# The last stores of a SiLU-multiply kernel, issued from SP instead of from ACT's queue

## The chip, the cores and the metric

The kernel runs on one core of a Trainium2 chip. The metric is the device time of one execution, in microseconds (us); lower is better. The span in a profile is some 1.8 us shorter than that time (470.1 against 471.92 us in the profiled run of before). Executions of one kernel differ by up to 0.8 us, so effects of some tenths of a us are read from the trace and not from the time.

Four names are used throughout. **ACT** is ScalarE and **DVE** is VectorE. **SP** is SyncE, which here only issues DMAs. A **ring** is the queue of transfers that one issuing engine has on the DMA engines: q1 in the profile belongs to SP, q10 to ACT.

## The reference

```python
def reference(x):                     # x: (32, 512, 2048) float32
    half_dim = x.shape[-1] // 2
    x1, x2 = x[..., :half_dim], x[..., half_dim:]
    return x1 * (1 / (1 + np.exp(-x1))) * x2      # (32, 512, 1024) float32
```

It reads 134.2 MB, writes 67.1 MB, and does one activation and one multiply per output.

## The kernel before

The rows are cut into 16 tiles of 8 MB in and 4 MB out. Two input and two output buffers exist. A tile is computed in four pieces of 2 rows per partition; its result is stored whole, except in the last tile, where each piece is stored as soon as it is done.

```python
    K, KC = 8, 2
    ...
    def load(i):
        xt = in_pool.tile([P, K, in_cols], dt, name="xt")
        nc.sync.dma_start(out=xt, in_=xv[i])
        loaded[i] = xt

    load(0); load(1)
    for i in range(n_tiles):
        xt = loaded.pop(i)
        last = i == n_tiles - 1
        ot = out_pool.tile([P, K, half], dt, name="ot")
        for c in range(0, K, KC):
            ce = c + KC
            nc.scalar.activation(out=ot[:, c:ce, :], in_=xt[:, c:ce, :half],
                                 func=mybir.ActivationFunctionType.Silu)
            nc.vector.tensor_mul(out=ot[:, c:ce, :], in0=ot[:, c:ce, :],
                                 in1=xt[:, c:ce, half:])
            if last:
                nc.scalar.dma_start(out=ov[i][:, c:ce, :], in_=ot[:, c:ce, :])
        if not last:
            nc.scalar.dma_start(out=ov[i], in_=ot)
        if i + 2 < n_tiles:
            load(i + 2)
```

The framework may reorder instructions of one engine where data allows it. In the program that results, ACT's queue holds for the last tile: activations 0 to 2, the stores of pieces 0 to 2, activation 3, the store of piece 3.

Of the kernel before, what the change touches and what calls it, by code (L numbers as in the profile page):

```python
# [1 line left out]

# [4 lines left out]


@with_exitstack
def kernel(  # L10
    ctx: ExitStack,
    tc: tile.TileContext,
    x: bass.AP,
    out: bass.AP,
):





    nc = tc.nc
    P = nc.NUM_PARTITIONS

    x_flat = x.flatten_outer_dims()
    out_flat = out.flatten_outer_dims()
    num_rows, in_cols = x_flat.shape
    half = in_cols // 2
    dt = x_flat.dtype

    K = 8  # L30
    KC = 2
    n_tiles = num_rows // (P * K)
    assert n_tiles * P * K == num_rows

    in_pool = ctx.enter_context(tc.tile_pool(name="in_pool", bufs=2))
    out_pool = ctx.enter_context(tc.tile_pool(name="out_pool", bufs=2))

    xv = x_flat.rearrange("(n p k) d -> n p k d", p=P, k=K)
    ov = out_flat.rearrange("(n p k) d -> n p k d", p=P, k=K)

    loaded = {}
# [6 lines that stand above are left out]
    load(0)  # L48
    load(1)
# [6 lines that stand above are left out]
            nc.scalar.activation(  # L56
                out=ot[:, c:ce, :],
                in_=xt[:, c:ce, :half],
                func=mybir.ActivationFunctionType.Silu,
            )  # L60
            nc.vector.tensor_mul(  # L61
                out=ot[:, c:ce, :],
                in0=ot[:, c:ce, :],
                in1=xt[:, c:ce, half:],
            )
            if last:
                nc.scalar.dma_start(out=ov[i][:, c:ce, :], in_=ot[:, c:ce, :])  # L67
        if not last:
            nc.scalar.dma_start(out=ov[i], in_=ot)
        if i + 2 < n_tiles:  # L70
            load(i + 2)


# [1 line left out]
_INS = ['x']  # L75
_OUTS = [((32, 512, 1024), 'float32')]


# [23 lines left out]
```

## Time and profile before

| what | value |
|---|---|
| time, median of 4 runs | 471.92 us (471.72 to 472.5) |
| bytes moved, mean rate | 201.35 MB, 428 GB/s |
| last load lands | 451.97 us from the span's start |
| previous tile's 4 MB store (the "old store") lands | 459.23 us |
| the last tile's pieces land | 461.65, 464.08, 466.51, 469.23 us |
| compute of the last tile ends (multiply 3) | 465.34 us |

Lines of the page of before: span; busy time of the engines; the busy tenths of the DMA engines in 40 slices of the span; the chain that ended last, by engine.

```profile
span 470.1 us, 267 instructions
...
DVE 142.4 (30%) x64; ACT 118.3 (25%) x65; POOL 0.2 (0%) x4
...
DMA  8999999999999999999999999999999999999998
...
DMA 80%; DVE 15%; ACT 4%; issue 0%; ACTq 0%; SPq 0%
```

The DMA engines are at nine tenths or more in 38 of 40 slices. That is the limit of this kernel: the compute engines are idle 70% and 75% of the time. Note the chain's 15% DVE: it means that the chain of releases passes through DVE, not that a faster DVE would help as long as the DMA engines always have other work.

The tail in the timeline of before (start, duration, engine, line, operation, tiles; in brackets the idle time before it and what ended it; ACTq is ACT's sequencer issuing a DMA):

```profile
452.05 5.51 ACT L56 ACTIVATE ot<-xt 128x2048 f32<-128x2048 f32 x3 [21.65 <-DMA xt<-in_x_dram]
453.99 6.70 DVE L61 TENSOR_TENSOR ot<-ot,xt 128x2048 f32<-128x2048 f32 x3 [20.06 <-ACT ot L56]
456.32 4.74 ACTq L67 DMA_DIRECT2D out_dram<-ot  x3
461.11 1.91 ACT L56 ACTIVATE ot<-xt 128x2048 f32<-128x2048 f32 x1 [3.54 <-DVE ot L61]
463.05 2.29 DVE L61 TENSOR_TENSOR ot<-ot,xt 128x2048 f32<-128x2048 f32 x1 [2.36 <-ACT ot L56]
465.37 0.34 ACTq L67 DMA_DIRECT2D out_dram<-ot  x1
```

Here the wait that the change aims at stands in plain sight. Activation 3 has its data since 451.97 us, but it stands in ACT's queue behind three store issues, each of which waits for a multiply. ACT idles 3.54 us, and then DVE idles 2.36 us.

The same tail seen from the DMA engines: the stretches view of before (stretch and length in us, busy time of DVE, ACT and POOL, TensorE clock, mean busy share of the 16 DMA engines, GB/s):

```profile
457.00:458.00 1.00, 1.00 (x1) 0.56 (x1) 0.00 (x0) 1.00 0.54 229
458.00:459.00 1.00, 1.00 (x2) 0.00 (x0) 0.00 (x0) 1.00 0.93 393
...
464.00:465.00 1.00, 1.00 (x1) 0.00 (x0) 0.00 (x0) 1.00 0.95 401
465.00:466.00 1.00, 0.34 (x1) 0.00 (x0) 0.00 (x0) 1.00 0.24 98
466.00:467.00 1.00, 0.00 (x0) 0.00 (x0) 0.00 (x0) 1.00 0.94 393
...
468.00:469.00 1.00, 0.00 (x0) 0.00 (x0) 0.00 (x0) 1.00 0.64 262
```

(A packet is counted where it starts, and the old store's packets are long, so the dip at 457 us is partly counting.) The DMA engines are kept busy through ACT's and DVE's idle time, from the stores already in the ring. Only at 465 to 466 us do they run dry. And the DMA issues of the page (KB each, median us from issue to landing) show the queueing:

```profile
out_dram<-ot ACTq DMA_DIRECT2D x15, 4096.0 KB, 39.7
out_dram<-ot ACTq DMA_DIRECT2D x4, 1024.0 KB, 5.4
```

A 1 MB piece takes 5.4 us (the median of the four) from issue to landing, though 1 MB at 430 GB/s is 2.4 us of transfer. The Trainium skill, page "Perfetto Trace Analysis", section "DMA Instruction — HWDGE (DVE, Sync)", warns that the window shown for a DMA instruction ends once its descriptors have been generated and the issuing engine is free again, and that the data movement is not in it. This trace agrees: the issue shows as 0.34 us, the landing comes 3.9 to 5.8 us after it.

### The profile page before, as it was taken

The page shows a single profiled execution, that of the slowest core. Times are in us where ns is not written, and L with a number is a line of the kernel's source. Part 1 is how long each engine was busy: PE and PEld are TensorE (multiplying, and loading weights), DVE is VectorE, ACT ScalarE, POOL GpSimd, SP SyncE. Part 2 cuts the span into 40 slices and gives each one's busy share as a digit, 9 for nine tenths or more (in the row PEclk, how much of TensorE's full clock was granted, in tenths as well). Part 3 has the DMA queues.
Part 4 walks back from the last instruction along what each step waited for, and adds up shares of the span by engine and source line. Part 5 has one row for each costly group of instructions (what it writes and reads, how often), then busy time and mean ns, then how long its engine had stood idle before and what let it go on. Part 6 is the DMA issues. An engine that isn't in the chain of part 4 may idle for free.

```text
span 470.1 us, 267 instructions
## 1 busy us (share of the span) xinstructions
DVE 142.4 (30%) x64; ACT 118.3 (25%) x65; POOL 0.2 (0%) x4
## 2 busy tenths in 40 slices
DVE  0070704207052070511606115070250702407033
ACT  1050506014060240602306032060320604106041
POOL 0000000000000000000000000000000000000000
DMA  8999999999999999999999999999999999999998
GB/s 357 446 446 401 401 485 435 418 401 443 449 446 401 441 457 396 446 474 390 468 404 438 457 441 407 427 420 449 446 410 432 480 401 418 440 474 424 399 424 337
DMA packets 5042, 201.35 MB, mean 428 GB/s; under 512 B 560, under 2 KB 560, under 8 KB 560
## 3 DMA queue, kind: packets, MB, share of 16 engines
q1 hardware_dynamic: 2304, 134.22, 66.2%
q10 hardware_dynamic: 2736, 67.11, 33.1%
q14 instruction: 2, 0.02, 0.0%
HBM read 134.22 MB, written 67.11 MB: 428 GB/s over the span
## 4 chain that ended last, share of the span: by engine, by line
DMA 80%; DVE 15%; ACT 4%; issue 0%; ACTq 0%; SPq 0%
DMA xt<-in_x_dram 80%; DVE ot L61 15%; ACT ot L56 4%; SPq L45 0%; ACTq L67 0%; ACTq L56 0%
## 5 line engine op out<-in xcount | busy, mean ns | idle before, releaser
L61 DVE TENSOR_TENSOR ot<-ot,xt 128x2048 f32<-128x2048 f32 x64 | 142.4, 2286 | 322.9 <-ACT ot L56 322.9
L56 ACT ACTIVATE ot<-xt 128x2048 f32<-128x2048 f32 x64 | 117.1, 1898 | 344.0 <-DMA xt<-in_x_dram 340.4
L56 ACT ACT_TABLE_LOAD x1 | 1.3, 1283 | 0.7 <-PEq L86 0.7
L86 POOL MEMSET const-bfloat16-1.0<- 128x1 bf16 x1 | 0.1, 101 | 0.0
L86 POOL MEMSET const-uint8-127<- 128x1 uint8 x1 | 0.1, 101 | 0.0
L86 POOL MEMSET const-float32-0.0<- 128x1 f32 x1 | 0.1, 98 | 0.2 <-issue 0.2
L86 POOL MEMSET const-float32-1.0<- 128x1 f32 x1 | 0.1, 98 | 0.0
## 6 DMA issues: line engine op xcount, KB each, us to landing
out_dram<-ot ACTq DMA_DIRECT2D x15, 4096.0 KB, 39.7
out_dram<-ot ACTq DMA_DIRECT2D x4, 1024.0 KB, 5.4
xt<-in_x_dram SPq DMA_DIRECT2D x16, 47.1
```

The lines of the kernel that those rows point to most:

```text
L56: nc.scalar.activation(out=ot[:, c:ce, :], in_=xt[:, c:ce, :half], func=mybir.ActivationFunctionType.Silu,)
L61: nc.vector.tensor_mul(out=ot[:, c:ce, :], in0=ot[:, c:ce, :], in1=xt[:, c:ce, half:],)
L86: nc = _bacc.Bacc("TRN2", target_bir_lowering=False, num_devices=1)
```

## The change

The intent is to free activation 3 from the store issues, so that compute ends earlier. The loads are all issued by then, so SP has nothing else to do.

```diff
             if last:
-                nc.scalar.dma_start(out=ov[i][:, c:ce, :], in_=ot[:, c:ce, :])
+                nc.sync.dma_start(out=ov[i][:, c:ce, :], in_=ot[:, c:ce, :])
```

(The changed file has one more blank line, so its line numbers are one higher.)

## The prediction

> **What bounds it.** The kernel moves 201.35 MB in a 470.1 us span, 428 GB/s on average, and the page shows the DMA engines at nine tenths or more in 38 of 40 slices; VectorE is busy 30%, ScalarE 25%. The chain of waits is 80% loads, 15% multiplies, 4% activations. Only the tail, after the last load lands at 451.97 us, is touched.
>
> **The tail now** (timeline from 452 us, and the stores' landings):
> - Activations 0 to 2 of the last tile run from 452.05 to 457.56; multiplies 0 to 2 end at about 456.3, 458.5 and 460.70, and ACT's queue issues their stores at 456.32, 458.52 and 460.72.
> - Activation 3 stands behind the third store in ACT's queue: ScalarE idles 3.54 us and starts at 461.11. VectorE then idles 2.36 us; multiply 3 runs 463.05 to 465.34 and its store goes out at 465.37.
> - The previous tile's 4 MB store lands at 459.2, 25.3 us after its issue. The pieces land 5.3, 5.6, 5.8 and 3.9 us after issue: at 461.65, 464.1, 466.5, 469.2. They follow each other by 2.43 us where they queue (1 MB at about 430 GB/s), the last by 2.73 us.
>
> **What the change does.**
> - Activation 3 no longer waits for a store issue: about 457.6 to 459.5. Multiply 3 starts when multiply 2 ends, 460.72, and ends at 463.0: compute ends 2.33 us earlier.
> - The last store goes out at about 463.03 from SP, idle since the last load's issue at 405.10. An issue costs 0.33 us on SP, 0.34 on ACT: nothing saved or added.
> - It moves no fewer bytes. In the stretches view the DMA engines move 393 to 442 GB/s from 458 to 465 us, 98 in 465 to 466, and 393 again until 468. The pieces already queue behind a backlog (issue to landing grows from 5.3 to 5.8 us); a store issued 2.33 us earlier mostly queues longer. The hole is some 0.7 us on most engines, but the engine that finishes last had its part of piece 2 done only at 466.5, after the last store's issue, so it hardly idled.
> - Expected landings: 461.65, 464.1, 466.5, then 466.5 + 2.43 = 468.9 instead of 469.2. Of 2.33 us about 0.3 us (at most the hole of 0.7) reaches the end. The 0.9 us from landing to the span's end stay.
> - The ring itself: by the Trainium skill, page "DMA: Bandwidth & Descriptors", section "Issuing engines are not separate DMA queues", SP's and ACT's transfers run on the same 16 DMA engines. No load is left in SP's ring, so I expect no effect from the ring. The trace of before cannot show this.
>
> **Predicted time:** 471.55 us, range 471.0 to 472.2 us. Chances: faster by over 2% 0.01, within 2% 0.98, slower by over 2% 0.01.
>
> **What would show each step.** Right: no idle time of ScalarE or VectorE over 0.1 us between the last tile's pieces; multiply 3 ends near 463.0; SP issues near 456.3, 458.5, 460.7, 463.0; no hole in the DMA rate between 458 and 468; the last piece takes nearly 6 us to land, not 3.9. Wrong: the last landing moves by over 1 us (then the hole counted, not the backlog), or piece 0 lands later than 461.7 (then the ring matters).
>
> **What would make it wrong.** Piece 0 on a separate ring could share the engines with the old store and shift the laggard engine by some tenths of a us; SP could react to VectorE's semaphore later; and runs differ by 0.8 us (471.72 to 472.5), more than the effect.

## The result, and the profile after

| | before | after |
|---|---|---|
| median, us | 471.92 (471.72 to 472.5, 4 runs) | 471.83 (471.73 to 472.15, 4 runs) |
| ratio | | 0.9997, 95% interval 0.998 to 1.0015 |

Ratios are the mean time of one kernel's fast runs over that of the other's of the same rounds, so not quite the ratio of the medians. The change makes no difference that can be measured in the time. The timeline of after:

```profile
451.97 7.31 ACT L57 ACTIVATE ot<-xt 128x2048 f32<-128x2048 f32 x4 [21.59 <-DMA xt<-in_x_dram]
453.91 8.90 DVE L62 TENSOR_TENSOR ot<-ot,xt 128x2048 f32<-128x2048 f32 x4 [20.00 <-ACT ot L57]
456.23 6.94 SPq L68 DMA_DIRECT2D out_dram<-ot  x4
```

The change did all that it was meant to do. The four activations and the four multiplies each run without a gap, and compute ends at 453.91 + 8.90 = 462.81 us instead of 465.34: 2.5 us earlier (0.08 us of it because the last load landed that much earlier in this execution). The stretches of after:

```profile
457.00:458.00 1.00, 1.00 (x1) 1.00 (x2) 0.00 (x0) 1.00 1.05 238
458.00:459.00 1.00, 1.00 (x2) 1.00 (x1) 0.00 (x0) 1.00 0.37 156
459.00:460.00 1.00, 1.00 (x1) 0.28 (x1) 0.00 (x0) 1.00 1.06 451
...
464.00:465.00 1.00, 0.00 (x0) 0.00 (x0) 0.00 (x0) 1.00 0.99 418
465.00:466.00 1.00, 0.00 (x0) 0.00 (x0) 0.00 (x0) 1.00 1.03 434
466.00:467.00 1.00, 0.00 (x0) 0.00 (x0) 0.00 (x0) 1.00 1.01 426
...
468.00:469.00 1.00, 0.00 (x0) 0.00 (x0) 0.00 (x0) 1.00 0.26 107
```

The hole at 465 us is gone (434 GB/s instead of 98). But a new, smaller one has come at 458 us (156 GB/s instead of 393), where the old store ends and piece 0 begins. The row for 457 us shows why: the engines count as busy (1.05) at only 238 GB/s, as some packets of piece 0 that began there took over 1 us. And the page's issues, SP's now:

```profile
out_dram<-ot ACTq DMA_DIRECT2D x15, 4096.0 KB, 39.7
out_dram<-ot SPq DMA_DIRECT2D x4, 1024.0 KB, 5.9
```

The pieces land 5.5, 5.8, 6.0 and 6.2 us after issue; before it was 5.3, 5.6, 5.8 and 3.9. So the last store is issued 2.53 us earlier and then takes 2.39 us longer (6.24 against 3.85). The last landing is at 469.08 us instead of 469.23.

Two questions follow. Is it really the backlog in the DMA engines that ate the gain? And what is the new hole at 458 us?

### The profile page after: what moved, and what is told of

The parts are those of the page before. It is cut to its first block, busy times and chain, and to the rows that moved or that the text cites. A ratio compares the mean times of both kernels' runs of the same rounds, so it can differ in the third digit from the quotient of the medians.

```text
span 470.0 us, 269 instructions
## 1 busy us (share of the span) xinstructions
DVE 142.4 (30%) x64; ACT 118.2 (25%) x65; POOL 0.2 (0%) x4
## 4 chain that ended last, share of the span: by engine, by line
DMA 80%; DVE 15%; ACT 3%; DVEq 0%; issue 0%; SPq 0%; ACTq 0%
DMA xt<-in_x_dram 80%; DVE ot L62 15%; ACT ot L57 3%; DVEq L98 0%; SPq L46 0%; ACTq L57 0%
```

## How the landings are read

A transfer is split over 16 DMA engines, and the trace records a completion from each, 16 per DMA. The table gives, for each kernel's profiled execution, how long after the old store piece 0 completes, and how long after the old store the last piece completes. "Mean" is over the 16 completions, "last" compares the last of them. The records do not name the DMA engine; that the last completions belong to the same engine is my reading of the spread, which stays nearly constant from DMA to DMA as long as they queue (1.25, 1.24, 1.20, 1.19 and 1.17 us in before, from the last load to piece 2). In after this does not hold: the spread falls from 1.00 us (old store) to 0.79 (piece 0). The engine that turned to piece 0 latest, at 458.70 us, was done with its first packet at 459.01, but one of the slow packets that are described below, begun at 457.85, ended only at 459.19; so another engine became the last one, by 0.17 us. "Slow packets" counts data packets of the pieces that took over 0.6 us; the others took about 0.31 us for 8 KB.

| kernel | piece 0 after old store: mean / last, us | last piece after old store: mean / last, us | slow packets |
|---|---|---|---|
| before | 2.45 / 2.43 | 10.76 / 10.00 | 0 |
| before, repeated | 2.46 / 2.43 | 10.70 / 10.02 | 0 |
| after | 2.99 / 2.63 | 10.31 / 9.94 | 9 |
| after, repeated | 3.18 / 2.48 | 10.49 / 9.81 | 15 |
| e1: ACT's ring, wait removed | 2.46 / 2.45 | 9.79 / 9.80 | 0 |
| e1, repeated | 2.46 / 2.43 | 9.79 / 9.71 | 0 |
| e2: SP's ring, wait kept | 3.21 / 2.55 | 10.82 / 9.86 | 14 |
| e_warm (has a 64 KB load between the two) | 2.74 / 2.60 | 10.15 / 9.95 | 1 |
| e_early (first piece half as large) | 1.14 / 1.10 | 9.73 / 9.69 | 0 |
| m_sp_sp | 2.46 / 2.45 | 9.79 / 9.72 | 0 |
| m_sp_act | 2.46 / 2.44 | 9.79 / 9.72 | 0 |
| f_sp_sp | 2.45 / 2.44 | 9.79 / 9.71 | 0 |

In e_warm the 64 KB load lands 0.20 us (mean) and 0.17 us (last) after the old store; counted from that load, the row reads 2.54 / 2.43 and 9.95 / 9.78.

The kernel ends with the *last* completion. Without any hole and without slow packets the last piece comes 9.7 to 9.8 us after the old store; in before it is 10.0. So in the last completion there were only 0.2 to 0.3 us to be had, 0.06% of the time. In the mean the hole of before is 1.0 us (10.76 against 9.79), but the kernel does not end with the mean.

## The experiments

### The change repeated, and before repeated

> The change once more, for the spread between executions and for a closer interval. If the slower start of piece 0 in SP's ring belongs to the change, piece 0 lands 2.6 us after the old store again and its first packets on several DMA engines take about 1.0 to 1.3 us; if it was chance, 2.42 us and 0.31 us. Time 471.8, ratio 0.9998.

> The kernel before once more, for the spread of the trace: tail 17.26 us within 0.1, piece 0 2.42 us after the old store, last piece 2.7 us after the third.

After: 471.97 us (471.69 to 472.32, 5 runs), before on the same chip 471.9; ratio 1.0001, interval 0.9989 to 1.0014. The slow first packets came again, on 15 of 16 engines (0.64 to 1.34 us). In the last completion piece 0 came after 2.48 us and not the 2.6 expected, so the loss on the last engine ranges from 0.05 to 0.2 us. Before came out as expected: its tail from load to last landing was 17.27 us against 17.25.

### e1_act_hoist and e1_again: the wait taken away, the ring kept

Edit against before, shortened: in the last tile the fourth activation stands ahead of the stores of pieces 1 to 3 in ACT's queue; all stores stay on ACT.

```diff
         for c in range(0, K, KC):
+            if last and c == 3 * KC: continue
             ... activation and multiply of piece c
-            if last: store piece c from nc.scalar
+            if last and c == 0: store piece 0 from nc.scalar
+        if last:
+            activation and multiply of piece 3
+            stores of pieces 1, 2, 3 from nc.scalar
```

> The wait taken away without changing the ring: all four stores stay on ACT's queue, but activation 3 stands ahead of the stores of pieces 1 to 3. Tail measured from the last load's landing to the last piece's landing: 17.26 us in before, 17.19 in after. Backlog theory (the DMA engines, not the compute, end the kernel; only the hole before the last piece comes back): compute ends 2.3 us earlier, the last piece takes about 6 us from issue to landing, pieces 1 to 3 land 2.43 us apart, tail about 16.95 us. If besides the change of ring costs something, piece 0 lands 2.42 us after the old store as in before, and this kernel's tail is 0.2 us shorter than that of after. Rival (the compute end is what counts and the ring of the loads ate the gain): tail shorter by some 2 us, 15.0 us. Rival (no effect of the ring, after's 2.63 us is chance): tail equal to that of after repeated. Time: backlog 471.6 us, ratio 0.9993; compute rival 469.7, ratio 0.995.

> The stores kept on ACT's queue with the wait taken away, once more, to see whether 0.9991 holds: ratio 0.9990 to 0.9998; no slow packets, piece 0 2.45 us after the old store in the mean, slowest engine 9.8 us from the old store to the end.

The timeline of e1, second half:

```profile
457.76 1.89 ACT L72 ACTIVATE ot<-xt 128x2048 f32<-128x2048 f32 x1
458.81 4.74 ACTq L84 DMA_DIRECT2D out_dram<-ot  x3
460.90 2.29 DVE L77 TENSOR_TENSOR ot<-ot,xt 128x2048 f32<-128x2048 f32 x1
```

The wait is gone on ACT's own queue too: changing two places in the order frees activation 3 as well as SP does. Times were 471.51 us (ratio 0.9991, interval 0.9978 to 1.0005) and 471.65 us (0.9997, interval 0.9983 to 1.001). Both intervals contain 1. The rival by which compute counts and SP's ring ate the gain would have needed 0.995. There are no slow packets and no hole, and the mean completion is 9.79 us after the old store, 0.5 to 0.7 us better than with SP. The tail from the last load's landing was 17.06 us, not 16.95, and so no shorter than that of the repeated after (17.06); that finer expectation missed in e1. In e1_again the tail was 16.95 us. It counts from the last load, whose own last completion varies by some tenths between executions.

### e2_ring_only: the ring changed, the wait kept

Edit against before:

```diff
+            if last and c == 3 * KC:      # one column that needs piece 2's multiply
+                nc.scalar.activation(out=ot[:, c:c+1, 0:1], in_=ot[:, c-KC:c-KC+1, 0:1], func=Silu)
             ... activation and multiply of piece c
-                nc.scalar.dma_start(out=ov[i][:, c:ce, :], in_=ot[:, c:ce, :])
+                nc.sync.dma_start(out=ov[i][:, c:ce, :], in_=ot[:, c:ce, :])
```

> The ring changed without taking the wait away: the stores go out from SP, but a one-column activation that reads piece 2's result holds activation 3 back as in before. If the ring has a cost of its own: piece 0 lands about 2.63 us after the old store, as in after, not 2.42. The last piece, issued near 465.5 into an idle ring, lands about 3.9 us later; tail 17.3 to 17.5 us, time 472.0, ratio 1.0002. If the ring costs nothing: piece 0 at 2.42 us, tail 17.26 plus the tiny activation's time.

471.92 us, ratio 1.0 (0.9987 to 1.0013). Piece 0 comes late as in after (14 slow packets, 3.21 us in the mean), so that belongs to the change of ring and not to the freed wait. The size was missed where it matters: the tail was 17.10 us and not 17.3 to 17.5. The wait is there as in before:

```profile
461.27 0.20 ACT L57 ACTIVATE ot<-ot 128x1 f32<-128x1 f32 x1 [3.16 <-DVE ot L67]
463.45 2.29 DVE L67 TENSOR_TENSOR ot<-ot,xt 128x2048 f32<-128x2048 f32 x1 [2.21 <-ACT ot L62]
```

Compute ends at 465.74 us, against 465.34 in before, but this execution's old store also landed later, by 0.54 us. Counted from the old store, the last store is issued 0.14 us earlier than in before (6.01 us after it, against 6.15) and lands 0.14 us earlier (9.86 against 10.00). In both it takes 3.85 us to land.

### s_before and s_after: the same change without a backlog

If the backlog hides the gain, the gain must appear when the backlog is taken away. In both kernels DVE makes each product of the last tile twice, once into space that is no longer needed; the result is unchanged. A piece then costs 4.6 us of DVE, more than the 2.4 us of its store. The order on ACT and DVE is pinned, so that activation 3 stands behind the third store in the one and not in the other; the cut below leaves the pinning out.

```diff
             if last:
+                nc.vector.tensor_mul(out=xt[:, c:ce, :half], in0=ot[:, c:ce, :], in1=xt[:, c:ce, half:])
             nc.vector.tensor_mul(out=ot[:, c:ce, :], in0=ot[:, c:ce, :], in1=xt[:, c:ce, half:])
```

> The kernel before with the backlog taken away, result unchanged: in the last tile VectorE also makes each piece's product once into space that is no longer needed, so a piece costs 4.6 us of VectorE instead of 2.3, more than the 2.43 us that the DMA engines take for its store. Stores on ACT's queue, activation 3 behind the third store as in before. Multiply 3 ends about 474.4 us, its store lands 3.9 us later, near 478.3; time about 481. To be compared with the next run.

> The same doubled VectorE work with the change (stores from SP, activation 3 free). Backlog theory: without a backlog the whole wait shows at the end, so this run is 2.3 us faster than the one with stores on ACT's queue (2.0 to 2.6 us), against 0.1 us in the real pair. Rival (the wait is worth nothing whatever the DMA engines do, or SP's stores are late by as much): within 0.3 us of it.

One stretch of the doubled kernel with ACT's stores, which shows that the DMA engines now run dry between pieces, and its last lines in the timeline:

```profile
462.00:464.00 2.00, 2.00 (x2) 0.00 (x0) 0.00 (x0) 1.00 0.01 4
```

```profile
468.26 1.91 ACT L59 ACTIVATE ot<-xt 128x2048 f32<-128x2048 f32 x1 [10.52 <-DVE ot L71]
470.21 2.29 DVE L66 TENSOR_TENSOR xt<-ot,xt 128x2048 f32<-128x2048 f32 x1 [2.36 <-ACT ot L59]
472.53 2.29 DVE L71 TENSOR_TENSOR ot<-ot,xt 128x2048 f32<-128x2048 f32 x1
474.86 0.34 ACTq L78 DMA_DIRECT2D out_dram<-ot  x1
```

The timeline of the doubled kernel with SP's stores, the last two multiplies:

```profile
467.77 2.29 DVE L66 TENSOR_TENSOR xt<-ot,xt 128x2048 f32<-128x2048 f32 x1
470.09 2.29 DVE L71 TENSOR_TENSOR ot<-ot,xt 128x2048 f32<-128x2048 f32 x1
```

DVE's idle time ahead of piece 3 is the same 2.36 us as in before. This time it reaches the end: 481.47 us against 479.02 us (all runs 481.09 to 481.57 and 479.0 to 479.11), a difference of 2.45 us (2.0 to 2.6 was expected). The last landing moves from 478.72 to 476.25 us. In both, the last store takes 3.84 to 3.86 us to land: the store before it had landed, so it waits for none. The same edit is worth 2.45 us here; in the real kernel no gain can be measured in the time, and the last completion comes 0.06 to 0.2 us earlier after the old store. The doubled work was put in to take the waiting stores away, and both kernels of this pair have it.

### f_sp_sp: compute made much earlier, with the bytes unchanged

The change, plus the previous tile's 4 MB store from SP as well. It now stands behind the last load in the same ring and no longer competes with it, so the last load lands earlier.

```diff
-            nc.scalar.dma_start(out=ov[i], in_=ot)
+            (nc.sync if i == n_tiles - 2 else nc.scalar).dma_start(out=ov[i], in_=ot)
```

> The change, and the previous tile's 4 MB store from SP too. It then stands behind the last load in the same ring, so that load should land some 4 us earlier, near 448 us, and the compute of the last tile end near 459 us, 6 us earlier than in before. Backlog theory: the end moves by no more than the 0.2 us that any gapless tail gains, last landing near 469.1, time 471.6 to 471.9, ratio 0.999 to 1.0. If compute still counted, the end would come 2 us or more earlier (ratio 0.995).

The timeline of f_sp_sp:

```profile
449.59 7.31 ACT L57 ACTIVATE ot<-xt 128x2048 f32<-128x2048 f32 x4 [19.00 <-DMA xt<-in_x_dram]
451.53 8.90 DVE L62 TENSOR_TENSOR ot<-ot,xt 128x2048 f32<-128x2048 f32 x4 [17.41 <-ACT ot L57]
453.85 6.94 SPq L68 DMA_DIRECT2D out_dram<-ot  x4
```

Compute ends at 460.43 us, 4.9 us earlier than in before (6 were expected; the load landed at 449.51 and not near 448). The last landing is at 468.90 us, 0.33 us earlier. The time is 471.52 us, ratio 0.9993 (0.9979 to 1.0007). It lies just below the 471.6 to 471.9 expected, and far above the 469.5 or so of the rival. Nearly 5 us of compute taken off the tail bought at most what closing the hole buys.

Put together, the last landings of all these runs follow from two limits, and the later one counts. One is the queue: 9.7 to 9.8 us after the old store (e1, f_sp_sp; 9.94 and 9.81 in the two executions of after, with their slow packets). The other is compute: 3.84 to 3.87 us after the issue of the last store (before, before repeated, e2, s_before, s_after). In before the compute limit is at 465.37 + 3.85 = 469.22 us and the queue's at about 459.22 + 9.75 = 468.97. So compute did set the end of before, but only by 0.25 us, and that is all that freeing activation 3 could gain. This is an account made after the runs, from their numbers.

### e_warm and e_early: what makes the first packets on SP's ring slow

In after, the first packet of piece 0 takes 0.98 to 1.33 us on the 9 engines that turn to it within 1.75 us of its issue, and 0.31 us on those that turn to it after 1.87 us or more. In e2 the border lies between 1.81 and 1.86 us. Two theories were set against each other. Both edits are against after, shortened:

```diff
 e_warm:
+            if last and c == 0:
+                nc.sync.dma_start(out=xt[:, 0:1, 0:128], in_=xv[i][:, 0:1, 0:128])
 e_early:
-        for c in range(0, K, KC): ce = c + KC
+        cuts = [0, 1, 3, 5, 7, 8] if last else [0, 2, 4, 6, 8]
+        for c, ce in zip(cuts, cuts[1:]):
```

> The change, and before the first store a load of 64 KB on SP's ring (the same values over values already used), issued when activation 0 ends, near 454 us, so that the ring was in use 2 us before piece 0. Theory A (the first packet is slow because the ring had been idle for 6 us): no packet of piece 0 over 0.6 us, mean landing of piece 0 2.45 us after the old store's, as on ACT's ring. Theory B (a packet is slow on each DMA engine that turns to piece 0 less than about 1.85 us after its issue, with another ring's packets under way until then): the slow packets stay, 9 to 15 of them, 2.99 to 3.2 us. Tail by the slowest engine unchanged within 0.15 us either way.

> The change with the last tile cut 1, 2, 2, 2, 1 rows instead of 2, 2, 2, 2, so that the first store leaves SP near 454.3 us, 3 us before the old store's data ends. Theory B (lateness of the issue): no, or few, first packets over 0.6 us besides what sharing with the old store's 32 KB packets costs, and no loss: mean finish of the engines 0.5 us earlier than in after, as in the run with the stores kept on ACT's queue and the wait taken away. Theory A (idle ring): the first packet of the small store is slow on most engines all the same, and the loss of 0.5 to 0.7 us in the mean stays. Time within 0.2% of before in both, as the slowest engine hardly idles: 471.5 to 471.8 us.

e_warm (one run, so its state is unknown, 472.87 us; its last tile began 0.9 us later than in before, ahead of the part looked at) had 1 slow packet and 2.54 us in the mean from the landing of its 64 KB load. Engines turned to piece 0 from 0.86 us after its issue on, and all but one were not slow: theory B as written is wrong. e_early (471.97 us where 471.5 to 471.8 was expected, ratio 0.9999, interval 0.9982 to 1.0016) had no slow packet although the ring had been idle, and the mean completion came 9.73 us after the old store, 0.6 to 0.8 us better than in after: theory A as written is wrong too. What fits both is that a packet is slow if it comes to a ring with nothing waiting in it *and* is issued late. In both experiments something had been waiting in SP's ring when the engines came to it.

e_early shows one thing more. Its first store was issued at 454.39 us, but its first packet began only at 457.74, when the first engines were done with the old store; 26 packets of the old store began after 455.5 us, over 1.1 us after that issue, while in s_after, where the engines were idle, a first packet began 0.84 us after its issue. So no engine took a packet of the new ring in between.

### m_sp_sp and m_sp_act: the rings changed over

All loads go from ACT and all stores from SP. The last pieces go from SP (m_sp_sp) or from ACT (m_sp_act, with the order of e1).

```diff
-        nc.sync.dma_start(out=xt, in_=xv[i])
+        nc.scalar.dma_start(out=xt, in_=xv[i])
 ...
-            nc.scalar.dma_start(out=ov[i], in_=ot)
+            nc.sync.dma_start(out=ov[i], in_=ot)
```

(In both, an ordering without a wait keeps the next tile's activations behind the load in ACT's queue.)

> The rings of the whole kernel changed over: all loads from ACT, all stores from SP, so the last pieces are in SP's ring behind the old store, as they are in ACT's ring in before. Theory C (the slow first packets come to a ring that held nothing when piece 0 was issued late, whichever ring it is): no packet of piece 0 over 0.6 us, mean landing of piece 0 2.45 us after the old store's. Rival S (it is SP's issuing that is slower): slow packets, 3.0 to 3.2 us, as in the change.

> All loads from ACT, the 4 MB stores from SP, the four last pieces from ACT, whose ring is empty then, with activation 3 ahead of the stores of pieces 1 to 3. Theory C: 9 to 15 packets of piece 0 over 0.6 us although ACT issues it, mean landing 2.9 to 3.2 us after the old store's. Rival S: none, 2.45 us.

No slow packet in either: 471.32 us and 471.25 us, one run each. For m_sp_sp this is what theory C says, and the rival S fails. For m_sp_act theory C fails: ACT's ring was empty, and nothing was slow. It fails narrowly, as the engines turned to piece 0 from 1.73 us after its issue on, at the border seen in after and e2 (packets that began 1.74, 1.75 and 1.81 us after the issue were slow there). The cause of the slow first packets therefore stays open. What is shown is only this: they came, in number, in the three executions in which piece 0 was issued late into SP's empty ring while the old store was still under way (9, 15 and 14), and in none of the others. An empty ring alone is not enough: in s_after SP's ring was empty too, the old store's data had been moved by the time the engines turned to it, and the first packets, 0.84 us after the issue, took 0.31 us. The slow packets cost 0.5 to 0.75 us in the mean and 0.05 to 0.2 us in the last completion.

The issues show one more sign. The issue of piece 1, the second store, took 0.84, 0.89 and 0.63 us in these three executions, 0.53 us in e_warm, and 0.65 us in m_sp_act, where ACT issued it. In all other runs it took 0.33 to 0.34 us. So in m_sp_act the change of ring did leave a mark on ACT's ring, though not on a packet. What links the two was not tested.

## Why the prediction was right

- **The total.** 471.55 us was predicted, with 471.0 to 472.2 as the range; 471.83 was measured. No difference clear of noise was forecast, and none was found. The number alone tests little: the range also holds before's own 471.92, so the steps below count for more.
- **Compute ends 2.33 us earlier.** Right: 2.5 us, and every gap of ACT and DVE between the pieces is gone. The four issues on SP came at 456.24, 458.44, 460.64 and 462.84 us, close to the 456.3, 458.5, 460.7 and 463.0 predicted.
- **The gain is lost in the backlog.** Right, and shown in three ways: with the backlog the change gives nothing that the time can show (0.15 us in the last landing), without it 2.45 us, and compute 4.9 us earlier gives 0.33 us in the last landing. The last piece takes 6.2 us to land, "nearly 6" was predicted.
- **The engine that finishes last hardly idled.** Right: gapless tails put the last completion 9.7 to 9.8 us after the old store, against 10.0 in before. The 0.3 us predicted is what e1 and f_sp_sp show in this measure (0.2 to 0.3 us); after itself shows 0.06 and, repeated, 0.2. The hole in the mean over the engines was 1.0 us and not the "some 0.7" predicted.
- **No effect from the ring.** This step was wrong. The prediction's own test, piece 0 later than 461.7 us, came true: 461.77 us, though the old store had landed 0.09 us earlier. The prediction "no hole between 458 and 468" failed for the same reason: the rate was 156 GB/s at 458 to 459. It rested on the Trainium skill, page "DMA: Bandwidth & Descriptors", section "Issuing engines are not separate DMA queues": DMAs from any engine run on the same 16 DMA engines, and issuing from several only saves issue time. In the time this holds (ratios 0.9997 and 1.0001). In the trace the change of ring has a cost of its own, which offset part of the 0.3 us: some 0.17 us in after, worked out above from its packets. "An issue costs 0.33 us on SP" failed once as well: the second issue took 0.84 us. That delayed nothing, as SP's next issue had to wait for a multiply until 460.64 us.

No version clearly beat before. e1, f_sp_sp and the two changed-over kernels gave medians or single runs of 471.25 to 471.65 us, but no interval excluded 1, and the two single runs have none.

## What to carry to other kernels

An idle gap on a compute engine in the tail is worth only what it starves: look at the DMA rate in the stretch after the gap, and at the time from issue to landing, before counting the gap as time. Compare that time with what the same store takes when no other is waiting (3.85 us here, of which 2.4 us are the bytes). If it takes longer, stores are queueing, and an earlier store mostly waits longer. The mean DMA rate can show a hole that the slowest of the 16 engines hardly had (1.0 us against 0.2 to 0.3 here), and the kernel ends with that one; and if an issue blocks an activation, try the order on the same queue before moving the issue to another engine.

## What the Trainium skill lacked or had wrong

- "DMA: Bandwidth & Descriptors", section "Issuing engines are not separate DMA queues", gives no cost for going over to another issuing engine's ring. Here the first 8 KB packet took 0.98 to 1.33 us instead of 0.31 us on 9 of 16 DMA engines in after (15 and 14 slow ones in two more executions), when the ring was SP's, empty, and the store issued under about 1.8 us before the engine turned to it from the old store. On ACT's ring, empty too (m_sp_act, 1.73 us and more, so at the border), no packet was slow, and the cause is open.
- The same page, section "Queues, rings and completion order", says that a DMA engine goes round the rings with work at packet granularity. With loads and stores both under way in mid-kernel the trace agrees: followed from the end of one packet to the start of the next, 64 KB and 32 KB packets of the two rings alternate (in before at 405.08, 407.49, 408.70 and 411.12 us). In e_early it did not show: a store issued on SP at 454.39 us got its first packet at 457.74, after the old store's packets.
- The same page, section "Anatomy of one DMA — SWDGE (gpsimd) path", puts most of a fixed 2 us down to the confirmation of the write. That fit is for another way of issuing; for these stores the last data packet ended at 468.88 us in before and the last completion came at 469.23, 0.35 us later (in after 468.69 and 469.08, 0.39 us).
- No page that I read gives a figure for how far the 16 engines drift apart: the completions of the old store spread over 0.82 to 1.98 us in these runs, more than the 0.3 us that the whole change could gain. "Perfetto Trace Analysis", section "What "DMA-bound" means", does name single DMA engines as a possible limit, which agrees.
